# A feed-forward up-projection on one Trainium2 core: half of its columns by seven block products instead of eight

## The chip, the core and the metric

The kernel runs on one core of one Trainium2 chip. The metric is the device time of one execution in microseconds (us). A core has five engines that run side by side, each through its own queue in order: TensorE (PE in the profile, its weight loads PEld), VectorE (DVE), ScalarE (ACT), GpSimd (POOL) and SyncE (SP), which here only issues DMAs. On-chip memory is SBUF (128 partitions) and PSUM, in which TensorE leaves its results: eight banks of 128 x 512 fp32.

## The reference

One encoder layer for 256 tokens of width 2048, all in fp32. Two mixing branches (a retention and a latent attention) are merged and added to the residual `h`; then comes the part that matters here:

```
z = _rmsnorm(h, norm_mlp_g) @ w_up           # (256 x 2048) @ (2048 x 8192)
h = h + square(relu(z)) @ w_down             # (256 x 8192) @ (8192 x 2048)
return _rmsnorm(h, norm_f_g)
```

## The kernel before

**Numbers.** An fp32 operand is split in two parts of TensorE's faster fp32r format: `hi` is the rounded value (ACT copies it, L151 or L216) and `lo` is what the rounding left (DVE subtracts, L152 or L217). A product is then three matmuls: hi by hi, hi by lo and lo by hi.

**Weights.** `weights` (L146) loads a piece of 128 x 1024 numbers (512 KB) into a `raw` tile (5 buffers) through SP's queue, and makes `hi` and `lo` of it (4 buffers each). All weights of the kernel go through this one stream.

**Two forms of a product.** In the *transposed* form (`t_unit`, L170) 128 output columns are made: the weights are the stationary operand and the activations of all 256 tokens move, hi and lo side by side. For each of the 16 blocks of the contraction there is one matmul 512 wide (weight hi by both, `t_pass1`, L159) and one 256 wide (weight lo by hi, `t_pass2`, L163). The result stands transposed (column on the partition, token on the free axis) in two halves of one PSUM bank, and `join` (L204) adds the halves: ACT copies one out (L206), DVE adds (L207). In the *natural* form (`n_tile`, L196; `down`, L807) a tile of 128 tokens is stationary and 512 weight columns move; the three matmuls are each 512 wide.

**Stages around the change.** `w_out` in natural form makes `hn` (L770 to L779: DVE adds the residual, ACT takes the sum of squares). `mlp_turn` (L757) transposes `hn` on TensorE, four 128 x 128 blocks to a PSUM bank, and splits the result into `hT`, scaled by the norm's gain. The up-projection (L785 to L800) is 64 transposed units `z0` to `z63`, each 16 + 16 matmuls; after `join`, DVE makes the squared ReLU in one operation (L800) into `hid`, which stays in SBUF. The down-projection (L819 to L832) runs over the 64 tiles of `hid`: split (`dh`, `dl`), two pieces of `w_down`, and 24 matmuls 512 wide into eight PSUM banks `pd` that are open all the way. Then comes the final norm.

**Memory.** Six SBUF tiles of 16 KB per partition (`big`, L100) hold activations in turn. PSUM is two pools of four banks, `mmps` (L133) and `atps` (L136).

**Order.** The program is traced in the order of the source. A planner then lists each engine's queue: it goes by priority in program order and by the times of its own durations at which operands and buffers come free (`schedule_with_timeline_sim`). On the chip each queue keeps that order.

Of the kernel before, what the change touches and what calls it, by code (L numbers as in the profile page):

```python
# [27 lines left out]
CHUNK = 64  # L28
DFF = 8192
FT = DFF // P  # L30
EPS = 1e-6
QK_SCALE = float(192.0 ** -0.5)
LOWEST = -3.4e38
# [55 lines left out]
def block_kernel(ctx: ExitStack, tc: tile.TileContext, A):  # L89
# [10 lines left out]
    def big(name, dt=F32, shape=(P, KT, S)):  # L100
        return act.tile(list(shape), dt, tag="act16", name=name)
# [31 lines left out]
    def mmps(name):  # L133
        return pmm.tile([P, 512], F32, tag="mm", name=name)
# [61 lines left out]
    def n_tile(out, w, x, t, k0, nk, start, stop):  # L196
        ts = slice(t * P, (t + 1) * P)
        for k in range(nk):
            PE.matmul(out, x.hi(k0 + k, ts), w[0][:, k], start=start and k == 0, stop=False)
            PE.matmul(out, x.lo(k0 + k, ts), w[0][:, k], start=False, stop=False)  # L200
        for k in range(nk):
            PE.matmul(out, x.hi(k0 + k, ts), w[1][:, k], start=False, stop=stop and k == nk - 1)

    def join(out, ps):  # L204
        t = sm.tile([P, S], F32, tag="join", bufs=2, name="join")
# [551 lines left out]
    def mlp_turn(c):  # L757
        for jj in range(2):
            pT = atps(f"ht{c}{jj}")
            for j in range(2):  # L760
                kt = 4 * c + 2 * jj + j
                for t in range(2):
                    o = j * S + t * P
                    PE.transpose(pT[:, o : o + P], hn[:, t, kt * P : (kt + 1) * P], ident)
                g = vec[:, V_MLP + kt : V_MLP + kt + 1]
                split(hT.hi(kt), hT.lo(kt), pT[:, j * S : (j + 1) * S], scale=g)
    hp = ctx.enter_context(tc.tile_pool(name="hp", bufs=1))
    ssh = cp.tile([P, 2, 4], F32, name="ssh")
    rh2 = cp.tile([P, 2], F32, name="rh2")
    for c in range(4):  # L770
        cs = slice(c * 512, (c + 1) * 512)
        pss = [mmps(f"wo{c}{t}") for t in range(2)]
        for kq in range(4):
            n_unit(pss, A["w_out"][4 * c + kq], mg, 4 * kq, 4, kq == 0, kq == 3)
            if kq == 0 and c:
                mlp_turn(c - 1)
        for t in range(2):
            V.tensor_tensor(out=hn[:, t, cs], in0=pss[t], in1=hn[:, t, cs], op=ALU.add)
            SC.activation(pss[t], hn[:, t, cs], AF.Square, accum_out=ssh[:, t, c : c + 1])  # L779
# [2 lines left out]
    V.tensor_scalar(rh2, rh2, 1.0 / D, EPS, op0=ALU.mult, op1=ALU.add)  # L782
    V.reciprocal(rh2, rh2)

    up = [mmps(f"z{i}") for i in range(2)]  # L785
    for i in range(2):
        t_half(up[i], A["w_up"][i], hT, 0)
        if i == 0:
            mlp_turn(3)
    hid = [big(f"hid{i}") for i in range(3)]  # L790
    hid.append(hp.tile([P, KT, S], F32, name="hid3"))
    for i in range(FT):
        if i < 2:
            pz = up[i]
            t_half(pz, A["w_up"][i], hT, 1)
        else:
            pz = mmps(f"z{i}")
            t_unit(pz, A["w_up"][i], hT)
        z = joined(pz)
        V.scalar_tensor_tensor(hid[i // KT][:, i % KT], in0=z, scalar=0.0, in1=z, op0=ALU.max, op1=ALU.mult)  # L800

    pd = [[(mmps if t == 0 else atps)(f"dn{t}{c}") for c in range(4)] for t in range(2)]
    ssf = cp.tile([P, 2, 68], F32, name="ssf")
    rf = cp.tile([P, 2], F32, name="rf")
    LAST = 2

    def down(i, t, c, w, hs):  # L807
        (hi, lo), (dh, dl) = w, hs
        ts = slice(t * P, (t + 1) * P)
        ws = slice(c % 2 * 512, c % 2 * 512 + 512)  # L810
        out = pd[t][c]
        end = i == FT - 1
        mm = tc.keep_in_program_order if i >= FT - LAST else (lambda ins: ins)
        mm(PE.matmul(out, dh[:, ts], hi[:, ws], start=i == 0, stop=False))  # L814
        mm(PE.matmul(out, dh[:, ts], lo[:, ws], start=False, stop=False))  # L815
        mm(PE.matmul(out, dl[:, ts], hi[:, ws], start=False, stop=end))  # L816

    tail = []
    for i in range(FT):  # L819
        dh = hp.tile([P, S], F32R, tag="dh", bufs=3, name=f"dh{i}")  # L820
        dl = hp.tile([P, S], F32R, tag="dl", bufs=3, name=f"dl{i}")
        split(dh, dl, hid[i // KT][:, i % KT])
        ws = []
        for half in range(2):
            w = weights(A["w_down"][i][:, half * 1024 : (half + 1) * 1024], [P, 1024])
            ws.append(w)
            if i < FT - LAST:
                for t in range(2):
                    for c in (2 * half, 2 * half + 1):
                        down(i, t, c, w, (dh, dl))  # L830
        if i >= FT - LAST:
            tail.append((i, ws, (dh, dl)))  # L832
# [7 lines left out]
    def finish(t, c, lo, hi, n):  # L840
        h = hn[:, t, c * 512 + lo : c * 512 + hi]
        ps = pd[t][c][:, lo:hi]
        V.scalar_tensor_tensor(h, in0=ps, scalar=rh2[:, t : t + 1], in1=h, op0=ALU.mult, op1=ALU.add)
        junk = hp.tile([P, 512], F32, tag="junk", bufs=2, name=f"junk{t}{n}")
# [37 lines left out]
def _n_units(w):  # L882
    k, n = w.shape
    u = w.reshape(k // 512, 4, P, n // 512, 512).transpose(3, 0, 2, 1, 4)
    return np.ascontiguousarray(u.reshape(-1, P, 4, 512))


def _cols(v):
# [57 lines left out]
```

## Time and profile before

| | us |
|---|---|
| median of 3 runs (1631.48 to 1631.87) | 1631.72 |
| the profiled execution | 1632.22 |
| its span, first to last instruction | 1630.4 |
| up-projection: first `z` matmul to first `dn` matmul | 915.5 to 1272.7 |
| down-projection: first to last `dn` matmul | 1272.7 to 1620.6 |

The span is shorter than the execution by 1.8 us, which lies around it. TensorE's granted clock has a mean of 0.998 of full speed. In the profile a line `L159 PE MATMUL z<-hT,hi ... x1024 | 245.5, 391` names the source line, engine, operation, the tile written and the tiles read, how many there were, the group's busy time in us and the mean duration of one in ns. TensorE's matmuls overlap: the duration of one is longer than the distance from its start to the next one's start, so rates are read from starts. In the timeline a line is start, duration, engine, line, operation, and in brackets how long the engine had been idle before it and what ended that.

### The profile page before, as it was taken

The page shows a single profiled execution, that of the slowest core. Times are in us where ns is not written, and L with a number is a line of the kernel's source. Part 1 is how long each engine was busy: PE and PEld are TensorE (multiplying, and loading weights), DVE is VectorE, ACT ScalarE, POOL GpSimd, SP SyncE. Part 2 cuts the span into 40 slices and gives each one's busy share as a digit, 9 for nine tenths or more (in the row PEclk, how much of TensorE's full clock was granted, in tenths as well). Part 3 has the DMA queues.
Part 4 walks back from the last instruction along what each step waited for, and adds up shares of the span by engine and source line. Part 5 has one row for each costly group of instructions (what it writes and reads, how often), then busy time and mean ns, then how long its engine had stood idle before and what let it go on. Part 6 is the DMA issues. An engine that isn't in the chain of part 4 may idle for free.

```text
span 1630.4 us, 23041 instructions
## 1 busy us (share of the span) xinstructions
PE 1614.9 (99%) x8782; PEld 1398.8 (86%) x8782; DVE 996.2 (61%) x1491; ACT 809.7 (50%) x1249; POOL 49.5 (3%) x62
## 2 busy tenths in 40 slices
PE   8999999999999999999999999999999999999997
PEld 6888888888889889888888888888888888888886
DVE  7974588655556658666765555555555555555555
ACT  6544555544445556765545544444444444444444
POOL 7100000000000000000000000000000000000001
PEclk9999999999999999999999999999999999999999
DMA  8665544555556554325575555555555655555553
GB/s 306 200 233 193 187 156 166 169 192 186 190 170 203 190 191 146 125 94 176 186 246 187 174 193 188 192 189 186 191 192 184 223 194 192 193 193 195 192 194 112
DMA packets 84480, 304.46 MB, mean 187 GB/s; under 512 B 9360, under 2 KB 9488, under 8 KB 83600
## 3 DMA queue, kind: packets, MB, share of 16 engines
q1 hardware_dynamic: 84368, 302.98, 55.3%
q8 instruction: 69, 1.13, 0.3%
q14 instruction: 43, 0.35, 0.1%
HBM read 300.84 MB, written 2.10 MB: 186 GB/s over the span
## 4 chain that ended last, share of the span: by engine, by line
PE 97%; DVE 1%; issue 0%; DMA 0%; ACT 0%; POOL 0%; SPq 0%; DVEq 0%; POOLq 0%; ACTq 0%
PE z L159 14%; PE z L163 8%; PE dn L816 7%; PE dn L814 7%; PE dn L815 7%; PE rg L159 4%; PE yr L159 4%; PE gr L159 4%; PE gm L159 4%; PE mo L159 4%; PE qk L159 2%; PE gr L163 2%; PE yr L163 2%; PE gm L163 2%; PE rg L163 2%; PE mo L163 2%
## 5 line engine op out<-in xcount | busy, mean ns | idle before, releaser
L152 DVE TENSOR_TENSOR lo<-raw,hi 128x1024 fp32r<-128x1024 f32 (+2 forms) x562 | 666.0, 1204 | 521.6 <-ACT hi L151 248.3
L151 ACT CAST hi<-raw 128x1024 fp32r<-128x1024 f32 (+2 forms) x562 | 580.8, 1035 | 536.9 <-PE z L159 135.2
L159 PE MATMUL z<-hT,hi 128*128 128x512 f32 x1024 | 245.5, 391 | 0.0
L159 PEld LDWEIGHTS z<-hT,hi 128*128 128x128 f32 x1024 | 188.0, 188 | 36.1
L815 PE MATMUL dn<-lo,dh 128*128 128x512 f32 x512 | 199.2, 389 | 0.0
L816 PE MATMUL dn<-hi,dl 128*128 128x512 f32 x512 | 199.2, 389 | 0.0
L814 PE MATMUL dn<-hi,dh 128*128 128x512 f32 x512 | 198.9, 389 | 0.0
L163 PEld LDWEIGHTS z<-hT,lo 128*128 128x128 f32 x1024 | 131.6, 191 | 5.1
L163 PE MATMUL z<-hT,lo 128*128 128x256 f32 x1024 | 133.1, 283 | 0.0
L815 PEld LDWEIGHTS dn<-lo,dh 128*128 128x128 f32 x512 | 96.1, 188 | 20.1
L816 PEld LDWEIGHTS dn<-hi,dl 128*128 128x128 f32 x512 | 96.1, 188 | 19.9
L814 PEld LDWEIGHTS dn<-hi,dh 128*128 128x128 f32 x512 | 96.1, 188 | 19.8
L216 ACT CAST dh<-hid 128x256 fp32r<-128x256 f32 x64 | 26.0, 407 | 89.3 <-PE dn L815 89.3
L159 PE MATMUL mo<-my,hi 128*128 128x512 f32 x256 | 65.5, 396 | 0.4 <-DVE val L207 0.4
L159 PE MATMUL rg<-x,hi 128*128 128x512 f32 x256 | 64.0, 395 | 0.0
L159 PE MATMUL yr<-ry,hi 128*128 128x512 f32 x256 | 61.4, 391 | 0.0
L159 PE MATMUL gr<-x,hi 128*128 128x512 f32 x256 | 61.3, 391 | 0.0
L159 PE MATMUL gm<-x,hi 128*128 128x512 f32 x256 | 61.1, 391 | 0.0
L159 PEld LDWEIGHTS gm<-x,hi 128*128 128x128 f32 x256 | 47.0, 188 | 9.1
L159 PEld LDWEIGHTS gr<-x,hi 128*128 128x128 f32 x256 | 47.0, 188 | 9.0
L159 PEld LDWEIGHTS yr<-ry,hi 128*128 128x128 f32 x256 | 46.9, 188 | 9.0
L159 PEld LDWEIGHTS rg<-x,hi 128*128 128x128 f32 x256 | 46.2, 188 | 8.6
(271 smaller groups left out, 2239.1 us busy)
## 6 DMA issues: line engine op xcount, KB each, us to landing
raw<-w_up SPq DMA_DIRECT2D x128, 512.0 KB, 4.2
raw<-w_down SPq DMA_DIRECT2D x128, 512.0 KB, 4.3
raw<-w_rv SPq DMA_DIRECT2D x32, 512.0 KB, 4.5
raw<-w_rg SPq DMA_DIRECT2D x32, 512.0 KB, 4.5
raw<-w_gret SPq DMA_DIRECT2D x32, 512.0 KB, 4.3
raw<-w_ret_o SPq DMA_DIRECT2D x32, 512.0 KB, 4.6
raw<-w_gmla SPq DMA_DIRECT2D x32, 512.0 KB, 4.4
raw<-w_out SPq DMA_DIRECT2D x32, 512.0 KB, 3.7
```

The lines of the kernel that those rows point to most:

```text
L151: SC.copy(hi, raw)
L152: V.tensor_tensor(out=lo, in0=raw, in1=hi.bitcast(F32), op=ALU.subtract)
L159: PE.matmul(out, w[0][:, k], x.both(k0 + k), start=start and k == 0, stop=False)
L163: PE.matmul(out[:, :S], w[1][:, k], x.hi(k0 + k), start=False, stop=stop and k == n - 1)
L216: SC.copy(hi, val)
L814: mm(PE.matmul(out, dh[:, ts], hi[:, ws], start=i == 0, stop=False))
L815: mm(PE.matmul(out, dh[:, ts], lo[:, ws], start=False, stop=False))
L816: mm(PE.matmul(out, dl[:, ts], hi[:, ws], start=False, stop=end))
```

## The change

The first 4096 of the 8192 columns of `w_up` are made in another form, and the other 32 units stay transposed units.

**Seven products.** For 1024 columns (`u`, four of them) and a pair of contraction blocks (`j`, eight of them) the activations are 2 x 2 blocks of 128 x 128 and the weights 2 x 2 blocks of 128 x 512. A scheme of Strassen's kind (Winograd's form) makes the 2 x 2 product out of seven block products of sums and differences. Each block product is three matmuls 512 wide, so one `s_step` has 21, into seven PSUM banks `qs` (products 3, 4, 2, 5 in `mmps`, 1, 6, 7 in `atps`) that stay open over the eight steps. `s_end` then makes the four output blocks `zo` of the seven banks, once for each `u`: one ACT copy and seven DVE operations of 128 x 512.

**The sums.** Those of the activations (`Combos.make`, four calls, each on DVE two operations of 128 x 1024, the split among them, and four of 128 x 256, and one ACT copy) are made once; two calls stand in the `w_out` stage, two among the first units. Those of the weights are made in every step on DVE: `fa` of 128 x 1024 and `fb` in two operations of 128 x 512. Then three pieces of 128 x 1024 and one of 128 x 512 are split.

**Turn and square.** The output is in natural form, so four turns for each `u` transpose it (four blocks each) in the middle of later steps. Squared ReLU is now two ACT operations (Relu, Square) for both forms, and ACT's queue issues a DMA that stores the tile in DRAM. The down-projection loads each pair of tiles back (`hl`, 3 buffers), first those of the old form, then the others.

**Order and memory.** Three old units come first (`EARLY`), then steps and old units alternate: 32 steps are spread over 27 units, so in five places two steps follow each other; two old units come last (`LATE`). The old units now use `atps` banks. `hn` is saved in DRAM by a DMA from ACT's queue and loaded back at the end of the stage, since its tile is used by `forms`. The sums' hi and lo have five buffers of their own each. The size of a DMA scratch area is reduced.

```diff
+    PRODUCTS = ((3, 0, 0), (4, 0, 1), (2, 1, 0), (5, 1, 1), (6, 2, 0), (1, 2, 1), (7, 3, 0))
...
+    def s_step(qs, src, x, j, between):
+        ra, rb = (wtile("raw", [P, 2, 512]) for _ in range(2))
+        nc.sync.dma_start(ra, src[:, :2])
+        nc.sync.dma_start(rb, src[:, 2:])
+        fa, fb = (forms[:, 2 * (j % 2) + i] for i in range(2))
+        V.tensor_tensor(out=fa, in0=rb[:, 1:].to_broadcast([P, 2, 512]), in1=ra, op=ALU.add)
+        V.tensor_tensor(out=fb[:, 0], in0=fa[:, 0], in1=ra[:, 1], op=ALU.add)
+        V.tensor_tensor(out=fb[:, 1], in0=fb[:, 0], in1=rb[:, 0], op=ALU.add)
+        ws = []
+        for i, r in enumerate((ra, fa, fb, rb[:, :1])):
...
+            split(hi, lo, r)
+            ws.append((hi, lo))
+        for n, (f, i, o) in enumerate(PRODUCTS):
+            if n == 4:
+                between()
+            (ah, al), (hi, lo) = x.get(f, j), ws[i]
+            first, last = j == 0, j == SJ - 1
+            PE.matmul(qs[f], ah, hi[:, o], start=first, stop=False)
+            PE.matmul(qs[f], al, hi[:, o], start=False, stop=False)
+            PE.matmul(qs[f], ah, lo[:, o], start=False, stop=last)
+
+    def s_end(qs, out, tmp):
...
+        SC.copy(t3, qs[3])
+        tt(e, qs[6], t3)
+        tt(f, qs[2], e, ALU.subtract)
+        tt(c21, qs[4], f)
+        tt(c11, qs[5], f)
+        tt(e, e, qs[5], ALU.subtract)
+        tt(c12, qs[1], e)
+        tt(c22, qs[7], t3)
...
+    def square(pair, n, val):
+        t = zp.tile([P, 2, S], F32, tag="hs", bufs=2, name=f"hs{pair}{n}")[:, : val.shape[1]]
+        SC.activation(t, val, AF.Relu)
+        SC.activation(t, t, AF.Square)
+        SC.dma_start(hid[pair][:, n : n + val.shape[1]], t)
...
+    for i in range(EARLY, FT - ST):
+        while done < SU * SJ and done * (FT - ST - EARLY - LATE) <= (i - EARLY) * SU * SJ:
+            next(steps)
+            done += 1
+        pz = atps(f"z{i}")
+        t_unit(pz, A["w_up"][i], hT)
+        square((ST + i) // 2, i % 2, joined(pz).unsqueeze(1))
+    for _ in steps:
+        pass
+    hn = big("hn2", shape=(P, 2, D))
+    nc.sync.dma_start(hn, keep)
...
-    for i in range(FT):
+    for n, i in enumerate((*range(ST, FT), *range(ST))):
+        if n % 2 == 0:
+            hl = hp.tile([P, 2, S], F32, tag="hl", bufs=3, name=f"hl{i}")
+            nc.sync.dma_start(hl, hid[i // 2])
```

More of the change, by code (lines that the diff above doesn't have):

```diff
@@ L30 @@
 FT = DFF // P
+SU = 4
+SJ = KT // 2
+ST = SU * 1024 // P
+EARLY, LATE = 3, 2
+SSF = 68
 EPS = 1e-6
@@ L204, in join, with tt @@
+    def s_end(qs, out, tmp):
+        t3, e, f = (tmp[:, i] for i in range(3))
+        c11, c12, c21, c22 = (out[:, t, c] for t in range(2) for c in range(2))
+        def tt(o, a, b, op=ALU.add):
+            V.tensor_tensor(out=o, in0=a, in1=b, op=op)
+        SC.copy(t3, qs[3])
[6 more added lines that the diff above has]
+        tt(c22, qs[7], t3)
     def join(out, ps):
@@ L776, in block_kernel @@
                 mlp_turn(c - 1)
+        if c in (1, 2):
+            hc.make(c - 1)
         for t in range(2):
@@ L783, in block_kernel @@
     V.reciprocal(rh2, rh2)
-    up = [mmps(f"z{i}") for i in range(2)]
-    for i in range(2):
-        t_half(up[i], A["w_up"][i], hT, 0)
+    hid = [hidd.tile([P, 2, S], F32, name=f"hid{i}") for i in range(FT // 2)]
+    zo = big("zo", shape=(P, 2, 4, 512))
+    def square(pair, n, val):
[3 more added lines that the diff above has]
+        SC.dma_start(hid[pair][:, n : n + val.shape[1]], t)
@@ new lines, in s_units, with turn @@
+    def s_units():
+        turns = []
+        for u in range(SU):
+            qs = {f: (mmps if f in (3, 4, 2, 5) else atps)(f"zs{u}{f}") for f in range(1, 8)}
+            for j in range(SJ):
+                s_step(qs, A["w_up_s"][u, j], hc, j, turns.pop(0) if turns and j else lambda: None)
+                yield
+            s_end(qs, zo[:, 0].rearrange("p (t c) n -> p t c n", t=2), zo[:, 1])
+            def turn(u, jj):
+                pT = atps(f"zt{u}{jj}")
+                for j in range(2):
+                    kt = 2 * jj + j
+                    for t in range(2):
+                        o = j * S + t * P
+                        src = zo[:, 0, 2 * t + kt // 4, kt % 4 * P : kt % 4 * P + P]
+                        PE.transpose(pT[:, o : o + P], src, ident)
+                square(4 * u + jj, 0, pT.rearrange("p (j n) -> p j n", j=2))
+            turns = [lambda u=u, jj=jj: turn(u, jj) for jj in range(4)]
+        for fn in turns:
+            yield
+            fn()
@@ L788, in block_kernel @@
+    forms = None
+    steps = s_units()
+    early = [atps(f"z{i}") for i in range(EARLY)]
+    for i, pz in enumerate(early):
+        t_half(pz, A["w_up"][i], hT, 0)
         if i == 0:
             mlp_turn(3)
-    hid = [big(f"hid{i}") for i in range(3)]
-    hid.append(hp.tile([P, KT, S], F32, name="hid3"))
-    for i in range(FT):
[L793 to L800, printed above, removed]
+            keep = hidd.tile([P, 2, D], F32, name="hnkeep")
+            SC.dma_start(keep, hn)
+            hc.make(2)
+            forms = big("forms", shape=(P, 4, 2, 512))
@@ new lines, in block_kernel @@
+    for i, pz in enumerate(early):
+        t_half(pz, A["w_up"][i], hT, 1)
+        square((ST + i) // 2, i % 2, joined(pz).unsqueeze(1))
+        if i == 0:
+            hc.make(3)
+    done = 0
+    for i in range(EARLY, FT - ST):
[4 more added lines that the diff above has]
+        t_unit(pz, A["w_up"][i], hT)
+        square((ST + i) // 2, i % 2, joined(pz).unsqueeze(1))
@@ L818, in block_kernel @@
     tail = []
-    for i in range(FT):
+    for n, i in enumerate((*range(ST, FT), *range(ST))):
+        if n % 2 == 0:
+            hl = hp.tile([P, 2, S], F32, tag="hl", bufs=3, name=f"hl{i}")
+            nc.sync.dma_start(hl, hid[i // 2])
         dh = hp.tile([P, S], F32R, tag="dh", bufs=3, name=f"dh{i}")
         dl = hp.tile([P, S], F32R, tag="dl", bufs=3, name=f"dl{i}")
-        split(dh, dl, hid[i // KT][:, i % KT])
+        split(dh, dl, hl[:, i % 2])
         ws = []
```

61 lines of the change are left out of this document (53 added, 8 removed).

## The prediction

> **What bounds the kernel now.** First the busy totals of the page, then the table by stage, then the timeline of two ordinary units.
>
> ```profile
> PE 1614.9 (99%) x8782; PEld 1398.8 (86%) x8782; DVE 996.2 (61%) x1491; ACT 809.7 (50%) x1249; POOL 49.5 (3%) x62
> ...
> 915.00:1272.00 357.00, 357.00 (x2054) 315.26 (x2053) 202.05 (x267) 162.52 (x203) 0.00 (x0) 1.00 0.56 189
> 1272.00:1620.00 348.00, 348.00 (x1540) 288.26 (x1540) 186.62 (x201) 155.07 (x201) 4.40 (x4) 1.00 0.56 187
> ```
>
> The stage lines hold the length and then the busy time of PE, PEld, DVE, ACT, POOL, the granted clock and the DMA share. In the up-projection (915 to 1272) PE is busy all the time at full clock, DVE 202 of 357 us, ACT 163, DMA 0.56: TensorE alone sets the end.
>
> ```profile
> 1004.76 2.36 DVE L152 TENSOR_TENSOR lo<-raw,hi 128x1024 fp32r<-128x1024 f32 x2 [2.41 <-PE z L163]
> 1005.46 3.82 PE L159 MATMUL z<-hT,hi 128*128 128x512 f32 x16
> 1005.66 0.37 ACT L206 COPY join<-z 128x256 f32<-128x256 f32 x1 [0.87 <-PE z L163]
> 1007.04 0.42 DVE L207 TENSOR_TENSOR val<-z,join 128x256 f32<-128x256 f32 x1
> 1007.49 0.42 DVE L800 SCALAR_TENSOR_TENSOR hid<-val 128x256 f32<-128x256 f32 x1
> 1009.11 2.08 PE L163 MATMUL z<-hT,lo 128*128 128x256 f32 x16
> 1011.03 1.32 PE L159 MATMUL z<-hT,hi 128*128 128x512 f32 x5
> ```
>
> Starts give the rates. Sixteen 512-wide matmuls take 1009.11 - 1005.46 = 3.65 us (228 ns each), sixteen 256-wide 1.92 us (120 ns): a unit is 5.57 us. DVE waits 2.41 us for PE to free a buffer: it is ahead, and has room.
>
> **What TensorE gains.** Thirty-two units go: 32 x 5.57 = 178.2 us. In come 4 x 8 steps of 21 matmuls 512 wide with activations stationary, the form of the down-projection:
>
> ```profile
> L814 PE MATMUL dn<-hi,dh x512: 389/389/396, 1272.7 to 1620.2; 128*128 128x512 f32 x171
> ...
> L816 PE MATMUL dn<-hi,dl x512: 388/389/389, 1273.1 to 1620.6; 128*128 128x512 f32 x171
> ```
>
> First to last start: (1620.6 - 1272.7) / 1535 = 226.6 ns. A step is 4.76 us, 32 steps 152.3: 25.9 us less. The 64 new transposes are priced by those of `hn`:
>
> ```profile
> 852.74 0.60 PE L764 MATMUL ht<-con,hn 128*128 128x128 f32 x4
> 853.10 0.48 PE L199 MATMUL wo<-hi,mg 128*128 128x512 f32 x1
> 853.41 0.40 PE L200 MATMUL wo<-hi,mg 128*128 128x512 f32 x1
> ```
>
> Four take 0.36 us, and the matmul behind them 0.31 instead of 0.23: 0.44 a turn, 16 turns 7.1 us. Net on TensorE: 25.9 - 7.1 = **18.8 us less**, a stage of 338.4 for 357.2. This holds if PE never waits.
>
> The Trainium skill ("TensorE: Matmul & The Clock Gate", section "Back-to-back issue gap") gives the isolated distance of matmuls at full clock as N/2.4 + 2.5 ns. That is 215.8 for 512 and 109.2 for 256; by it the estimate would be 166.4 - 145.0 = 21.4 saved instead of 25.9. The rows are slower than the rule in both forms, and more so in the form that goes.
>
> **What VectorE gets.** Distances between starts where DVE has no gap, from the end of the previous stage and the start of this one:
>
> ```profile
> 931.48 1.22 DVE L152 TENSOR_TENSOR lo<-raw,hi 128x1024 fp32r<-128x1024 f32 x1
> 932.61 0.42 DVE L800 SCALAR_TENSOR_TENSOR hid<-val 128x256 f32<-128x256 f32 x1
> 932.95 0.42 DVE L207 TENSOR_TENSOR val<-z,join 128x256 f32<-128x256 f32 x1
> ...
> L778 DVE TENSOR_TENSOR hn<-wo,hn x8: 683/688/692, 846.5 to 915.7; 128x512 f32<-128x512 f32 x8
> ```
>
> An operation of 128 x 1024 lasts 1.22 but the next starts after 1.13; 128 x 256 lasts 0.42 and occupies 0.34; 128 x 512 lasts 0.69 and, by the same 0.09, occupies 0.60. An operation that needs the one before it waits the full duration and 0.03 more (L207 to L800 above: 0.45). So a step is `fa` 1.25 + `fb` 0.72 + 0.60 + three splits of 1.13 + one of 0.60 = 6.56 us, against 4.76 of PE: **DVE can't feed steps alone**. A unit is 2.27 + 0.42 = 2.7 (the squared ReLU leaves DVE) against 5.57. `s_end` is seven operations, mostly in a chain, 4.6; each `make` 4.0. The stage: 32 x 6.56 + 32 x 2.7 + 4 x 4.6 + 2 x 4.0 + 3.8 (`hT`, `hn`, the sums) = 326.5 us against PE's 338.4: **DVE is 96% full**, where it was 57%.
>
> ACT: steps 32 x (3 x 1.05 + 0.62) = 121; units 32 x (2.10 + 0.37 + two squares' halves at 0.41) = 105; turns 16 x 1.2 = 19; the rest 7; 48 DMA issues at the 0.33 that SP's take = 16. That is 268 of 338, 79%. Queued behind each store on ACT are the next `hi` copies, for which DVE's `lo` waits; the 70 us of room cover it. If ACT were late, DVE would be, and PE with it.
>
> **Where PE will wait.** A wait can't be below nothing, and nothing in the sum is saved twice, so these only take from 18.8.
> - Start. Three early units and `mlp_turn` give PE 17.6 us. DVE has in that time six `lo` 6.8, three joins 1.2, two `make` 8.0 and 3.8 of the rest: 19.8, and then the first step's 6.6, of which the first products need 1.1. `forms` also waits until `hn` is stored: 2 MB, by `hn<-x` 8.8 us to landing, by the slower `xn<-x` (1 MB) 12.9; it ends about when needed. Between 0 and 5 us; I take 3.
> - Ends of a `u`. 4.6 us of DVE come at once. An old unit stands between, so the banks are free in time; DVE's lead, about 2 us with these buffers, and 0.65 of room in each pair of step and unit leave up to 2. Three inner ends: 0 to 6; I take 4.
> - Turns. Products 1, 6, 7 hold three `atps` banks, so units and turns share one. After a unit PE has four products (2.7 us) until the turn: ACT's copy (up to 1.05 behind another, then 0.37) and DVE's add (up to 1.13, then 0.42) make up to 3.0, typically 2. After the turn three products (2.0 us) cover Relu (up to 1.05, then 0.6). 16 turns, I take 0.1 each, 2; the far end is a rival.
> - End of the stage: four last turns and their banks before `pd`: 0 to 2; I take 1.
>
> Sum 10: a stage of 348.5, 8.8 us less than before.
>
> **Edits at nothing.** The two `make` in `w_out`: DVE is busy there 50 of 91 us; they borrow two of five `raw` buffers, and the three left hold 3 x 2.7 us of matmuls against 3.7 to landing. Without that cover, up to 4 us each. Storing and loading `hid`: 256 KB lands in 2.5 us (`out<-hn`), the first `hl` was stored hundreds of us earlier, and DMA has 0.44 of its time free; if not, a few us at the join of the stages. Reloading `hn` has the whole down-projection; SP's `raw` loads are queued behind it, and it waits for a freed tile, which the planner places after the combos' last use; five loaded buffers cover it. The scratch size moves no instruction.
>
> From the execution's 1632.2: 1632.2 - 18.8 + 10 = 1623.4; the median of the runs lies 0.5 below the profiled one, so **1623**.
>
> **Rivals.**
> 1. *All waits hidden*: 1631.7 - 18.8 = 1613, up to 1618. For it: in 15 to 25 us of the span DVE was busy 5.00 of every 5.00 us, so it can run without a gap. Against it: 4% of room.
> 2. *DVE becomes the bound.* Without the overlap of 0.09 between operations, because waits on ACT stand between them, the durations count: steps 32 x 6.95, units 32 x 2.87, `s_end` 4 x 4.8, the rest 12.3: 346 us, 8 above PE's sum; with gaps of 1 to 4% 350 to 360, against 357. Time 1624 to 1635, middle 1629. For it: such an order alternates ACT and DVE in every split. The Trainium skill ("VectorE: DVE Perf Modes", section "The DRAIN you can't avoid") says that the next operation starts only when the pipe is empty, and in the next section that an operation which isn't held starts earlier; the pairs of `lo` above (two in 2.36, not 2.45) agree with the exception.
> 3. *Slower, by the shared bank.* The queues' order is fixed beforehand. If on DVE a unit's `join` stands behind a step's block of forms and splits, rather than behind one operation, the bank comes free 0.2 + 1.4 + (3 to 6.6) + 0.4 after the unit, 2.3 to 5.9 us after PE wants it. The point from which it decides is 18.8 / 16 = 1.2 us a turn, less what the other waits took: 0.5. At 1.5 to 2.5 in each of 16 turns, 24 to 40 us: 1637 to 1660, middle 1645. Against it: the planner's queue puts a ready `join` first, as 933 us shows, where `join` came between two `lo`.
>
> That PE's products aren't seven but as slow as eight is excluded by counts: 672 matmuls of a known rate.
>
> **How the numbers follow.** Forecast (waits 5 to 14) 0.45; rival 1 0.12; rival 2 0.20; rival 3 0.23. The measurement tells about 0.2%, 3.3 us, from no change. Faster by more than that (below 1628.4): all of rival 1, the forecast, and a little of rival 2: 0.60. Within: 0.13. Slower: rival 3 and the end of rival 2: 0.27. The range 1613 to 1645 leaves out the upper half of rival 3 and the end of rival 1. Within the sign that I forecast, 1613 to 1628.
>
> **What would show it.** The `zs` matmuls' starts 227 ns apart, 672 of them; the up-projection about 348 us; PE's idle time named after DVE `lo`, `forms` or `val`, some 10 us, clustered at the start and at the three ends of a `u`; DVE's busy time in the stage 320 to 330. A stage below 343 is rival 1; DVE without gaps and PE waiting all along is rival 2; PE waiting at the turns' `zt` for `val`, over 1 us each, is rival 3. Waits outside the stage, in `w_out` or the down-projection, would make the forecast wrong in a place that I priced at nothing.

## The result and the profile after

| | before | after |
|---|---|---|
| median (runs) | 1631.60 us (4) | 1646.20 us (4, 1644.47 to 1648.04) |
| ratio | | 1.0091, 95% interval 1.0075 to 1.0107: 0.9% slower |
| profiled execution, its span | 1632.22, 1630.4 | 1647.19, 1645.4 |
| first `z` to first `dn` | 357.2 | 370.8 |
| first to last `dn` | 347.9 | 350.7 |

The forecast was 1623 in a range of 1613 to 1645. The time went the other way, 14.6 us up, and lies 1.2 us outside the range. The up-projection was to become 348.5 us; it is 370.8, and the down-projection gave 2.8 more.

The busy totals of the page after:

```profile
PE 1610.9 (98%) x8494; PEld 1374.6 (84%) x8494; DVE 1118.6 (68%) x1607; ACT 888.2 (54%) x1385; POOL 49.8 (3%) x62
```

TensorE has 288 matmuls fewer, but the span is longer. The stages, with the same columns as in the prediction (length, busy time of PE, PEld, DVE, ACT, POOL, clock, DMA share, GB/s):

```profile
915.00:1285.00 370.00, 349.54 (x1761) 290.25 (x1760) 315.84 (x366) 232.88 (x327) 0.00 (x0) 0.99 0.67 222
1285.00:1636.00 351.00, 349.70 (x1543) 288.33 (x1541) 184.77 (x200) 159.99 (x211) 4.78 (x5) 1.00 0.65 207
```

PE was busy for all of 357 us before; now it idles 20 of 370, while DVE has gone from 202 to 316 busy and still has 54 free. No engine is full: the loss is waiting. A stretch of TensorE's timeline shows that the matmuls cost what was said where nothing waits:

```profile
1149.41 0.39 PE L266 MATMUL zs<-shi,hc 128*128 128x512 f32 x1
1149.64 0.39 PE L265 MATMUL zs<-shi,hc 128*128 128x512 f32 x1
1149.86 0.39 PE L266 MATMUL zs<-shi,hc 128*128 128x512 f32 x1
```

Starts are 0.23 apart. What is new is in the groups (operation, count, busy time and mean ns of one, idle time before them):

```profile
L265 PE MATMUL zs<-shi,hc 128*128 128x512 f32 x96 | 39.0, 406 | 6.8 <-ACT shi L297 6.1 <-DVE zo L274 0.7
L266 PE MATMUL zs<-shi,hc 128*128 128x512 f32 x96 | 37.9, 395 | 0.0
```

PE idles mostly ahead of the *first* matmul that needs a step's split weights (L265; L266, which follows it, has no idle time). Its waits in the stage, by what ended them (total, times, longest):

```profile
PE zs L265 <- ACT shi L297: 6.1, 6, 3.0
PE z L164 <- ACT hs L877: 3.8, 5, 1.2
PE zs L267 <- DVE lo L298: 2.4, 4, 1.1
PE zs L265 <- ACT hi L297: 2.2, 3, 1.3
PE zs L267 <- DVE slo L298: 1.4, 3, 0.6
...
PE zt L897 <- ACT hs L877: 1.2, 1, 1.2
...
PE z L164 <- DVE val L288: 0.2, 1, 0.2
```

No name holds most of it. **To add it up without names**, take each distance between two starts on TensorE, subtract the rate of the first (0.228 and 0.120 in a unit, 0.2266 in a step, 0.44 for a turn), and sum from the first `z` to the last instruction of the stage. Before, that sum is -1.0; after, it is **32.1 us**, where the prediction had 10. The gaps over 0.7 us, sorted by the wait that ended them: start of the stage 3.0; splits of a step (`shi`, `slo`, `hi`, `lo`) away from the start 8.7; the shared bank after a turn (`hs`) 5.2; ends of a `u` 1.9. The other 13 are in gaps under 0.7. The sum also holds what a lower granted clock took, since the rates are those of the full clock; in the kernel after that is about 3 us, by an estimate from the clock rows at the end of this document.

The worst place shows how one wait leads to the next (start, duration, engine, and in brackets the wait):

```profile
1152.71 0.33 SPq L245 DMA_DIRECT2D raw<-w_up_s  x1
...
1154.40 0.60 PE L897 MATMUL zt<-con,zo 128*128 128x128 f32 x4
...
1155.85 0.59 ACT L877 ACTIVATE hs<-zt 128x512 f32<-128x512 f32 x1
...
1156.50 0.66 PE L897 MATMUL zt<-con,zo 128*128 128x128 f32 x4 [1.23 <-ACT hs L877]
...
1157.78 1.23 DVE L247 TENSOR_TENSOR forms<-raw,raw 128x1024 f32<-128x1024 f32 x1 [1.93 <-DMA raw<-w_up_s]
...
1159.04 1.04 ACT L297 CAST shi<-forms 128x1024 fp32r<-128x1024 f32 x1 [1.94 <-DVE forms L247]
...
1160.14 0.79 PE L265 MATMUL zs<-shi,hc 128*128 128x512 f32 x1 [2.99 <-ACT shi L297]
```

Two turns stand with one matmul between them. Both need the one bank that the products leave, so the second waits until Relu has emptied it. TensorE's queue then stands at a step whose weights were asked for at 1152.71 and landed at about 1157.7; one sum on DVE and one copy on ACT later TensorE goes on, 3 us late. The granted clock was 0.67 in the 5 us behind this place (same columns as the stages; the clock is the third figure from the end):

```profile
1155.00:1160.00 5.00, 0.92 (x6) 0.42 (x4) 3.07 (x3) 3.03 (x5) 0.00 (x0) 0.98 0.93 345
1160.00:1165.00 5.00, 4.86 (x15) 3.90 (x16) 3.71 (x5) 2.72 (x5) 0.00 (x0) 0.67 0.64 217
1165.00:1170.00 5.00, 5.00 (x31) 4.44 (x30) 2.16 (x3) 2.38 (x4) 0.00 (x0) 1.00 0.03 7
```

At the end of the stage, ACT stands for a store (`hs` has two buffers), and TensorE for ACT:

```profile
1287.10 0.84 ACTq L879 DMA_DIRECT2D hid<-hs  x2
...
1292.92 0.60 ACT L877 ACTIVATE hs<-zt 128x512 f32<-128x512 f32 x1 [5.33 <-DMA hid<-hs]
...
1293.57 0.50 PE L948 MATMUL dn<-hi,dh 128*128 128x512 f32 x1 [0.95 <-ACT hs L877]
...
1296.95 0.50 PE L948 MATMUL dn<-hi,dh 128*128 128x512 f32 x1 [0.35 <-ACT hs L877]
```

The first `dn` matmuls wait twice for a bank that Relu has to empty, and Relu for the store. The two places cost 1.6 us over the rate, and the last turn, which now stands among the `dn` matmuls, 0.4: most of the 2.8 us that the down-projection became longer.

### The profile page after: what moved, and what is told of

Same layout as the page of the kernel before. It is cut to its first block, busy times and chain, and to the rows that moved or that the text cites. A ratio compares the mean times of both kernels' runs of the same rounds, so it can differ in the third digit from the quotient of the medians.

```text
span 1645.4 us, 22858 instructions
## 1 busy us (share of the span) xinstructions
PE 1610.9 (98%) x8494; PEld 1374.6 (84%) x8494; DVE 1118.6 (68%) x1607; ACT 888.2 (54%) x1385; POOL 49.8 (3%) x62
## 5 line engine op out<-in xcount | busy, mean ns | idle before, releaser
L157 DVE TENSOR_TENSOR lo<-raw,hi 128x1024 fp32r<-128x1024 f32 (+2 forms) x498 | 591.1, 1202 | 378.9 <-ACT hi L156 246.0
L156 ACT CAST hi<-raw 128x1024 fp32r<-128x1024 f32 (+2 forms) x498 | 512.3, 1032 | 421.3 <-PE dn L950 95.3
L164 PE MATMUL z<-hT,hi 128*128 128x512 f32 x512 | 125.8, 397 | 5.3 <-ACT hs L877 3.8
L164 PEld LDWEIGHTS z<-hT,hi 128*128 128x128 f32 x512 | 96.7, 191 | 28.5 <-ACT hs L877 5.9
L297 ACT CAST shi<-forms 128x1024 fp32r<-128x1024 f32 x64 | 66.9, 1049 | 33.4 <-DVE forms L247 21.4
L298 DVE TENSOR_TENSOR slo<-forms,shi 128x1024 fp32r<-128x1024 f32 x64 | 77.9, 1219 | 5.9 <-ACT shi L297 5.9
L168 PEld LDWEIGHTS z<-hT,lo 128*128 128x128 f32 x512 | 66.2, 191 | 2.8
L168 PE MATMUL z<-hT,lo 128*128 128x256 f32 x512 | 67.2, 283 | 0.0
L297 ACT CAST hi<-raw 128x1024 fp32r<-128x1024 f32 x64 | 52.9, 834 | 26.3 <-PE z L164 15.4
L298 DVE TENSOR_TENSOR lo<-raw,hi 128x1024 fp32r<-128x1024 f32 x64 | 59.7, 952 | 3.4 <-PE z L168 3.0
```

Source lines behind the costliest of these rows:

```text
L156: SC.copy(hi, raw)
L157: V.tensor_tensor(out=lo, in0=raw, in1=hi.bitcast(F32), op=ALU.subtract)
L164: PE.matmul(out, w[0][:, k], x.both(k0 + k), start=start and k == 0, stop=False)
L168: PE.matmul(out[:, :S], w[1][:, k], x.hi(k0 + k), start=False, stop=stop and k == n - 1)
```

## The experiments

The expectations name theories by letters. The missing time is due to: **A** too few `raw` buffers; **B** stores that hold ACT through the two `hs` buffers; **C** DVE being nearly full; **D** the loads of `hl` standing early in SP's queue; **E** an order planned with loads that land sooner than they do; and, formed on the traces with three and two `u`, **F** the one PSUM bank that units and turns share.

"Lost" is the sum defined above, from each kernel's profiled execution, as is the last column; the median is that of all runs. Where the text says how many of TensorE's 8494 matmuls "moved", it is the smallest number that has to change places to turn one trace's order of starts into the other's.

| kernel | median us | ratio to before (95%) | lost us | first `z` to last `dn` |
|---|---|---|---|---|
| after | 1646.2 | 1.0091 (1.0075 to 1.0107) | 32.1 | 721.5 |
| four store buffers | 1640.8 | 1.0057 (1.0042 to 1.0072) | 28.8 | 715.9 |
| `hl` loads late | 1659.1 | 1.0173 (1.0156 to 1.0190) | 43.8 | 732.8 |
| six `raw` buffers | 1646.6 | 1.0090 (1.0075 to 1.0105) | 30.3 | 717.6 |
| no sums on DVE | 1644.1 | 1.0079 (1.0064 to 1.0094) | 31.4 | 719.2 |
| steps' weights loaded once | 1643.2 | 1.0070 (1.0055 to 1.0085) | 28.2 | 716.7 |
| three `u` | 1672.3 | 1.0252 (1.0234 to 1.0269) | 55.0 | 747.0 |
| two `u` | 1708.4 | 1.0470 (1.0454 to 1.0486) | 83.1 | 780.6 |
| TensorE in program order | 1669.4 | 1.0228 (1.0212 to 1.0244) | 50.2 | 737.8 |
| six product banks | 1631.3 | 0.9998 (0.9989 to 1.0008) | 15.8 | 703.9 |
| six banks, two `u` | 1635.4 | 1.0018 (1.0008 to 1.0027) | 8.7 | 705.7 |
| join by ACT | 1654.6 | 1.0137 (1.0122 to 1.0153) | 38.0 | 727.3 |
| join by ACT, two `u` | 1688.1 | 1.0349 (1.0331 to 1.0366) | 60.6 | 757.6 |
| turns together | 1666.1 | 1.0211 (1.0196 to 1.0226) | 54.4 | 740.9 |
| same, four store buffers | 1663.0 | 1.0190 (1.0175 to 1.0205) | 46.9 | 733.4 |
| six banks, four store buffers | 1630.2 | 0.9995 (0.9985 to 1.0006) | 15.7 | 703.1 |
| same, no sums on DVE | 1641.0 | 1.0058 (1.0039 to 1.0078) | 28.3 | 715.5 |
| half banks | 1652.5 | 1.0134 (1.0117 to 1.0151) | 24.1 | 722.5 |
| seventh product apart | 1640.7 | 1.0062 (1.0048 to 1.0076) | 26.6 | 714.0 |

### Buffers and loads

**Four store buffers.**

```diff
-        t = zp.tile([P, 2, S], F32, tag="hs", bufs=2, name=f"hs{pair}{n}")[:, : val.shape[1]]
+        t = zp.tile([P, 2, S], F32, tag="hs", bufs=4, name=f"hs{pair}{n}")[:, : val.shape[1]]
```

> The store's tile hs gets four buffers instead of two; nothing else is changed. Theory B (two store buffers: Relu waits on ACT until a store has landed, 4 to 6 us, and holds a PSUM bank and ACT's queue meanwhile) expects the 7.9 us of PE's gaps that end with hs in the up-projection and the 2.8 us that the down-projection became longer to go, and some that hang on them: 1632 to 1637. Theory A (five raw buffers are too few, so that VectorE stands for loads) expects the 2.8 us at the stage's end at most: 1642 to 1645. Theory C (VectorE, 96% full, can absorb no wait from anywhere) expects the same as A.

It took 5.4 us off, less than B expected and more than A and C, 2.2 of them in the down-projection (348.5). Only some 45 matmuls moved, so this is the cleanest of the edits: the stores were a cause, and about a third of the loss against before.

**Late `hl` loads.**

```diff
-            nc.sync.dma_start(hl, hid[i // 2])
+            tc.keep_in_program_order(nc.sync.dma_start(hl, hid[i // 2]))
```

> The loads of hl are kept behind all loads of the up-projection in SP's queue; three of them stood early in it, where SP waited 11.3 us in all for stores. Theory D (weight loads are late because SP waits behind those) expects the waits of the stage's first 60 us to shrink by about 5: 1640 to 1642. Theories A, B and C expect less than 3: 1643 to 1647.

Up to the last `z` the stage is as long as before the edit (368.2 for 369.4 us); then the first `dn` matmul waits 11.9 us for `dh`, since the loads now come too late. Where they had stood had cost little. D falls.

**Six `raw` buffers.**

```diff
-        dt, bufs = (F32, 5) if kind == "raw" else (F32R, 4)
+        dt, bufs = (F32, 6) if kind == "raw" else (F32R, 4)
```

> Six raw buffers instead of five. Theory A expects VectorE's 26.5 us of waits for loads to fall to a third and PE's gaps that end with shi, slo or lo, 15 us, to halve: 1634 to 1639. Theory B expects no change beyond 2 us: 1644 to 1647. Theory C expects a small gain: 1641 to 1645.

Nothing changed in the time, though some 220 matmuls moved. DVE waited 29.2 us for the steps' loads, where it had waited 26.5: a sixth buffer doesn't shorten that wait, and A falls as it was drawn.

**Weights of the steps loaded once** (two loads fewer in every later step; the two tiles that hold them take room, so four `raw` buffers are left for the units).

```diff
-        dt, bufs = (F32, 5) if kind == "raw" else (F32R, 4)
+        dt, bufs = (F32, 4) if kind == "raw" else (F32R, 4)
...
-        ra, rb = (wtile("raw", [P, 2, 512]) for _ in range(2))
-        nc.sync.dma_start(ra, src[:, :2])
-        nc.sync.dma_start(rb, src[:, 2:])
+        if not held:
+            held.extend(zp.tile([P, 2, 512], F32, name=f"held{i}") for i in range(2))
+            nc.sync.dma_start(held[0], src[:, :2])
+            nc.sync.dma_start(held[1], src[:, 2:])
+        ra, rb = held
```

> The steps' weights are loaded once and used in all 32 steps (the output is not the reference's): 62 of the up-projection's 128 loads are left out, VectorE, ScalarE and TensorE do all their work. Theory E expects the waits that hang on step loads to go, 20 of 32 us: up-projection 350, time 1625 to 1632. Theory C expects little: 1641 to 1646. Theory B (stores) expects its 5 to stay in both.

3 us. The DMA share of the stage fell to 0.38, and 28.2 us are still lost. So the late landing in the timeline above is one link of that chain; without any late step load nearly as much is lost, by other waits. E falls as the one cause.

### VectorE's load

The three sums of a step are left out.

```diff
-        V.tensor_tensor(out=fa, in0=rb[:, 1:].to_broadcast([P, 2, 512]), in1=ra, op=ALU.add)
-        V.tensor_tensor(out=fb[:, 0], in0=fa[:, 0], in1=ra[:, 1], op=ALU.add)
-        V.tensor_tensor(out=fb[:, 1], in0=fb[:, 0], in1=rb[:, 0], op=ALU.add)
...
-        for i, r in enumerate((ra, fa, fb, rb[:, :1])):
+        for i, r in enumerate((ra, ra, rb, rb[:, :1])):
```

> The three operations on VectorE that make the weights' sums are left out, and loaded pieces are split in their place (the output is not the reference's). VectorE loses 32 x 2.57 = 82 us of the stage's 327. Theory C expects the gaps at steps to go and the stage to come near 345: 1617 to 1624. Theory A expects half of the gaps at steps to stay, since pieces are held shorter but the loads are as many: 1630 to 1636. Theory B expects the 10 us at stores to stay: 1633 to 1638.

The same 350 us of the kernel after, of this one, and of the one with weights loaded once:

```profile
915.00:1265.00 350.00, 329.54 (x1645) 272.56 (x1644) 301.79 (x349) 221.83 (x310) 0.00 (x0) 0.99 0.66 219
```

```profile
915.00:1265.00 350.00, 329.99 (x1649) 274.68 (x1647) 229.43 (x253) 217.38 (x310) 0.00 (x0) 0.99 0.66 221
```

```profile
915.00:1265.00 350.00, 332.88 (x1663) 277.82 (x1662) 302.45 (x351) 222.42 (x311) 0.00 (x0) 0.98 0.38 128
```

DVE (third busy time) has 72 us less to do in the second line, and PE is busy 0.45 us more. The time is 20 us above C's range, and above A's and B's too: taking work off DVE doesn't bring the time down, so C falls as the one cause. The edit does more than that, though. A step's first copy on ACT (`shi`) now reads the loaded piece itself, and waited 56.3 us for loads, so this kernel may stand at another limit; what a lighter DVE is worth by itself, it doesn't tell.

### Fewer steps

```diff
-SU = 4
+SU = 3
```

> Three of the eight blocks of columns in the new form instead of four (24 steps over 35 units). By the rows PE's sum of the up-projection is 343 us and VectorE's 291 (85% instead of 96%). Theory C (VectorE's fill decides) expects most of the waits to go: up-projection 350, time 1624 to 1630. Theory E (waits come with each step, about 1 us, because the queues' order is planned with loads that land sooner than on the chip, whatever room VectorE has) expects 24 us of waits: up-projection 367, time 1639 to 1644.

> Two of eight blocks in the new form (16 steps over 43 units). PE's sum is 348 us, VectorE's 256 (73%). Theory C expects 2 to 4 us of waits: up-projection 351, time 1624 to 1628. Theory E expects 16 us of waits: 364, time 1636 to 1641.

Both are far outside what C and E expected: with three and two `u`, DVE's load falls (250 and 203 of the same 350 us), and the time *rises*, to 1672 and 1708. The trace with two `u` shows a unit straight behind a unit, which the kernel after hardly has:

```profile
994.84 2.07 PE L168 MATMUL z<-hT,lo 128*128 128x256 f32 x16
...
996.95 0.37 ACT L287 COPY join<-z 128x256 f32<-128x256 f32 x1 [0.86 <-PE z L168]
...
998.33 0.42 DVE L288 TENSOR_TENSOR val<-z,join 128x256 f32<-128x256 f32 x1
...
998.80 1.48 PE L164 MATMUL z<-hT,hi 128*128 128x512 f32 x5 [1.89 <-DVE val L288]
```

The bank of the first unit must be joined before the second can begin. From the first unit's last phase to the second's first matmul it is 3.96 us, for 1.92 of work: **2.04 us for handing the bank over**. That is theory F. TensorE's largest waits in this kernel, by name; `val` is the bank's, `shi` and `slo` are a step's splits:

```profile
PE zs L265 <- ACT shi L297: 17.1, 10, 3.3
PE z L164 <- DVE val L288: 14.1, 9, 1.9
PE zs L267 <- DVE slo L298: 10.1, 10, 1.8
PE zt L897 <- DVE val L288: 5.1, 4, 1.9
```

### TensorE in program order

Every matmul of a step and a unit, and every turn, is pinned to the order of the source.

```diff
-            PE.matmul(qs[f], ah, hi[:, o], start=first, stop=False)
+            pin(PE.matmul(qs[f], ah, hi[:, o], start=first, stop=False))
...
-                        PE.transpose(pT[:, o : o + P], src, ident)
+                        pin(PE.transpose(pT[:, o : o + P], src, ident))
```

> TensorE's queue is kept in the order of the source from the first step on: steps and units whole, none mixed. If the waits come from products that the planner put ahead of a ready unit, they go by half: 1630 to 1638. If what is late is the supply of sums and splits itself (theory C), a whole unit no longer fills a step's wait and the time rises or stays: 1645 to 1655.

18 us more lost, and 23.2 us more time with the same work and the same buffers, beyond both numbers expected: the order alone is worth that much. Now the shared bank's own names carry the waits, as the prediction's rival 3 drew them:

```profile
PE zt L901 <- DVE val L292: 11.3, 6, 3.1
PE z L168 <- DVE val L292: 9.5, 7, 2.6
PE zs L271 <- DVE slo L302: 4.4, 3, 2.2
PE zs L269 <- DVE zo L278: 4.1, 4, 2.4
```

Free to choose, the planner puts matmuls of later products in these places. The likely reading is that it escapes the wait for `val` at the price of standing at a step's splits earlier, which is where the kernel after shows its waits; the two traces fit it, and the next runs test it.

### A second bank

Product 7 is added into product 1's bank: TensorE's instructions are the same, and two banks are left for units and turns.

```diff
-            qs = {f: (mmps if f in (3, 4, 2, 5) else atps)(f"zs{u}{f}") for f in range(1, 8)}
+            qs = {f: (mmps if f in (3, 4, 2, 5) else atps)(f"zs{u}{f}") for f in range(1, 7)}
+            qs[7] = qs[1]
...
-            first, last = j == 0, j == SJ - 1
+            first, last = j == 0 and f != 7, j == SJ - 1 and f != 1
```

> Product 7 is added into the bank of product 1 (the output is not the reference's); every engine has the same instructions, but the steps hold six PSUM banks, and units and turns share two instead of one. Theory F (the one bank that units and turns share sets the order of TensorE's queue and its waits; a unit straight behind a unit costs 2.04 us) expects 10 to 20 of the 32 us of waits to go: up-projection 350 to 360, time 1625 to 1636. Theories C and E, in which sums and loads come late, expect 1642 to 1647.

> Two of eight blocks in the new form, with product 7 in the bank of product 1 (output not the reference's). With one shared bank this division took 1708 us. Theory F expects that a second bank takes nearly all of it away: up-projection 350 to 356, time 1625 to 1632, better than any so far. Theories C and E expect 1690 or more.

With four `u` 14.9 us less than the kernel after, as F expected; with two `u` 72.9 less than its counterpart, 3.4 above F's range and 55 below the other theories'. TensorE's waits with two `u`, all of them:

```profile
PE zs L265 <- ACT shi L297: 1.9, 1, 1.9
PE zs L265 <- ACT hi L297: 1.4, 1, 1.4
PE zs L267 <- DVE slo L298: 1.1, 1, 1.1
PE z L164 <- ACT hi L156: 0.6, 1, 0.6
PE z L164 <- DVE hT L301: 0.6, 1, 0.6
```

Not only `val` is gone; the 17.1 us for `shi` and 10.1 for `slo` are 1.9 and 1.1. Waits that bear a split's name went with the bank. For two `u` theory F is shown. The Trainium skill ("Perfetto Trace Analysis", section "Matmuls") asks for just this, that independent groups of matmuls rotate through different banks, so that emptying one lies beside filling the next; the two runs agree, by 72.9 us. The bank is enough to explain four `u` too, but a new order was drawn along with it: some 380 matmuls moved.

With four store buffers added:

> Product 7 in product 1's bank (output not the reference's), and four store buffers. With two it took 1631.3. Theory B for the rest: 4 to 6 us less, 1625 to 1627. If the stores only cost where the bank was short: 1629 to 1632.

1630.2: four store buffers are worth 5.4 us where the bank is short, and 1.1, within the scatter of the runs, where it isn't. Then the sums on DVE are left out as well:

> As six_hs4, and the three sums of the weights on VectorE left out (output not the reference's). Theory C, hidden so far behind the bank: the waits left, about 10 us, go too and the up-projection nears 341: 1615 to 1619. If VectorE's fill isn't the cause: within 3 us of six_hs4.

This is outside both expectations. With a second bank and 81 us less on DVE the time went *up* by 10.8 us, and 28.3 are lost. Two things changed. Some 290 matmuls moved. And what stood for the loads is another engine, for much longer; first a line of the kernel with sums, then one of the kernel without (total, times, longest):

```profile
DVE forms L247 <- DMA raw<-w_up_s: 24.6, 18, 3.9
```

```profile
ACT shi L294 <- DMA raw<-w_up_s: 85.9, 45, 6.5
```

With the sums, their first one waits for the load on DVE; without them, ACT's first copy does, and all of ACT's queue behind it. Whether the order or these waits took the 10.8 us, no run here separates. Since the kernel in program order shows that an order alone can be worth 23 us, differences of some 10 us between two edits that re-draw it say little by themselves.

### Handing the bank over sooner

ACT copies the whole bank, so that DVE's addition isn't needed to free it.

```diff
+        if whole[0]:
+            SC.copy(t, ps)
+            V.tensor_tensor(out=out, in0=t[:, :S], in1=t[:, S:], op=ALU.add)
+            return
```

> From the first step on, a unit's join copies the whole bank out with one ACT operation of 128 x 512 (about 0.6 us instead of 0.37) and DVE adds the halves in SBUF, so that the shared bank is free without DVE. Theory F expects 4 to 10 us less: 1636 to 1642. Theories C and E expect no change or 1 us more, for ACT's longer operation: 1645 to 1648.

> Two of eight blocks in the new form, with the join's copy of the whole bank by ACT. Theory F: a unit straight behind a unit waits about 1 us instead of 2: 1708 falls by 20 to 40, to 1668 to 1688. Theories C and E: 1705 to 1710.

With two `u` 20 us came back, at the edge of what F expected; with four `u` it is 8.4 us slower than the kernel after, against what F expected, and 38.0 us are lost. There the order put the first `dn` ahead of the last unit; what made it slower isn't shown.

All four turns of a `u` together, straight behind `s_end` (first as it is, then with four store buffers):

```diff
-                s_step(qs, A["w_up_s"][u, j], hc, j, turns.pop(0) if turns and j else lambda: None)
+                s_step(qs, A["w_up_s"][u, j], hc, j, lambda: None)
...
-            turns = [lambda u=u, jj=jj: turn(u, jj) for jj in range(4)]
-        for fn in turns:
-            yield
-            fn()
+            for jj in range(4):
+                turn(u, jj)
+            yield
```

> The four turns of a block stand together right after its end, when the seven banks are free, and no longer in the middle of the next block's steps; nothing else is changed. If the turns are the dear users of the shared bank, 10 to 14 of the 32 us go: 1632 to 1637. If the units are, little changes: 1642 to 1648.

> The same, and four store buffers instead of two. The two effects add: between0's time less 4 to 6, so 1627 to 1632 if the turns are dear, 1637 to 1642 if the units are. Below 1628 it would beat both kernels.

20 and 17 us slower than the kernel after, both outside what was expected. The four turns follow each other on one bank, `s_end` has to be finished for them, and the next step waits for `s_end` too (`zo` below). How the 20 us divide isn't shown. The largest waits of the first of the two:

```profile
PE zs L267 <- DVE lo L298: 7.9, 9, 2.3
PE zs L265 <- DVE zo L274: 6.0, 3, 3.4
PE zs L265 <- ACT shi L297: 4.8, 5, 1.9
```

### A second place without leaving anything out

**Half banks.** Units and turns in halves of the one bank, with four store buffers.

```diff
+    def h_unit(out, src, x):
...
+            for k in range(HK):
+                kk = half * HK + k
+                PE.matmul(out, hi[:, k], x.hi(kk), start=kk == 0, stop=False)
+                PE.matmul(out, hi[:, k], x.lo(kk), start=False, stop=False)
...
+        return halves[0][:, nh[0] % 2 * S : nh[0] % 2 * S + S]
```

> A second place in the one free bank, with nothing left out of the computation: from the fourth old unit on, a unit is made in half a bank (256 columns) by three matmuls 256 wide for each of its 16 blocks, so that units and turns take the two halves of the bank in turn, and a unit needs no join at all; turns become half turns of two transposes, at two points of a step; store buffers are four. TensorE's sum grows: 29 units x 16 x (3 x 120 - 348 = 12 ns) = 5.6 us, and the half turns some 1.3, together 7 against the kernel with four store buffers (1640.8). Theory F (the one bank for units and turns is what the time goes to): the 10.6 us that a second bank brought to the kernel with four store buffers come back: 1633 to 1639. Rival (the second bank helped only because another queue order was drawn, or one half can't be filled while the other is read): no gain, only the 7: 1646 to 1655.

1652.5, in the rival's range. The loss went from 28.8 us to 24.1, by less than the 7 us of added work; the rest of the 11.7 between the two medians isn't accounted for. The trace shows that the premise was wrong:

```profile
1148.67 0.38 PE L906 MATMUL halves<-con,zo 128*128 128x128 f32 x2
...
1149.09 0.38 ACT L889 ACTIVATE hs<-halves 128x256 f32<-128x256 f32 x1 [1.08 <-PE halves L906]
...
1149.52 0.44 PE L906 MATMUL halves<-con,zo 128*128 128x128 f32 x2 [0.47 <-ACT hs L889]
```

The second half turn starts only when Relu has read the *other* half: in this program a bank is one place, however it is cut. The Trainium skill ("PSUM — Partial Sum Buffer", section "PSUM bank collisions raise a hardware error") gives a reason for such waits: two engines must not access one bank on the same partitions at once, disjoint columns included. The wait of 0.47 us agrees with a program that keeps to it; what happens without the wait, no run here shows.

**The seventh product apart.** Product 7 leaves the steps and is made once for each `u` as a unit of 24 matmuls in a shared bank; ACT copies it out, and the last addition of `s_end` takes it.

```diff
+                if j == 5:
+                    s_seventh(atps(f"zs{u}7"), zo[:, 0, 3], u, hc)
+                    yield
...
-        tt(c22, qs[7], t3)
+        tt(c22, c22, t3)
```

> A second bank with nothing left out: of the seven products, product 7 leaves the steps (18 matmuls each, into six banks) and is made once for each 1024 columns as a unit of its own, 24 matmuls 512 wide in one of the two shared banks, behind the sixth step; ACT copies its bank to SBUF, where the last addition takes it. TensorE does the same 672 matmuls. Its weights are loaded a second time (8 MB more in all, on a DMA share of 0.66), VectorE's splits are the same columns in fewer operations, ACT does four copies more. Store buffers are four. Theory F (the one bank for units and turns is what the time goes to, whatever order is drawn): near the kernel with six banks and four store buffers, 1626 to 1634, TensorE's waits in the up-projection 10 to 18 us. Rival (six banks gained by the order that was drawn, not by the bank): near the kernel with four store buffers alone, 1638 to 1650, waits of 25 or more.

1640.7, the rival's number, 0.1 us from the kernel with four store buffers. It isn't a clean test. This kernel asks for 8 MB more and has four store buffers, and ACT's waits in the stage are new ones (in the kernel after the same two names have 4.4 and 4.1 us):

```profile
ACT hi L156 <- DMA raw<-w_up: 28.6, 19, 3.0
ACT hi L311 <- DMA raw<-w_up_s: 17.3, 11, 3.2
```

ACT waits 46 us for weights where it waited 8.5. Either that ate the bank's gain, or at four `u` the bank gains less than the six-bank kernels show; this run can't tell. No version without anything left out was faster than before; the best are this one and the one with four store buffers, both 0.6% slower.

## Why the prediction was wrong

**TensorE's sum, right.** 672 matmuls came in, and where nothing waits they start 0.23 us apart; with the loss taken off, the stage is 370.8 - 32.1 = 338.7 for the 338.4 predicted. As the loss is counted from the prediction's own rates, this confirms the counts and that no other work stands in the stage. TensorE has 18.8 us less to do, as predicted.

**VectorE's and ScalarE's load, nearly right.** 316 us busy for 320 to 330; ScalarE 233, where 252 were worked out besides the DMA issues. Rival 2 had DVE without gaps, and it idles 54 us of the stage: it isn't the bound. How much its fill adds to the waits stays open, since the kernels without sums stand for loads instead.

**The failed step: "Where PE will wait", a sum of 10.** By its items, in gaps over 0.7 us: start 3.0 for 3; ends of a `u` 1.9 for 4; turns 5.2 for 2 ("16 turns, I take 0.1 each"). The items that were named came out near their sum, 10.1 for 9. What was missing is a term for *ordinary steps*: 8.7 us of visible waits for a step's splits and 13 in small gaps; the end of the stage, taken at 1, cost 2.8, in the down-projection. The prediction had let DVE run ahead there because its total fitted. A total of 96% says nothing of when an operation stands in its queue: DVE waited 26.5 us in 17 places for weights to land, and ACT 21.4 for DVE's sums. No one of these waits is the cause: with the steps' loads left out, 28.2 us were still lost. Of the 13 in small gaps, about 3 are the halved clock (estimate below).

**An edit priced at nothing: storing `hid`.** DMA's free time was named as its cover, and it wasn't the issue. The buffer was: `hs` has two, a store took 3.8 us (128 KB) or 4.7 (256 KB) to land in the median, ACT's queue stood behind it for up to 5.33, and four buffers take 5.4 us off where the bank is short. ACT's "70 us of room" is no cover for a queue that goes in order.

**Rival 3, by its number but not by its sign.** Its middle of 1645 was 1 us from the result. Its sign, PE waiting at the turns for `val` by over 1 us each, isn't there: for `val` units waited 0.2 us in all, and one turn 1.2, for Relu. The bank it named is the strongest cause that the runs found (14.9 and 72.9 us when a second is free), but with a planner that may move other products ahead, the wait for the bank seems to turn into waits for splits: with the order pinned the sign is there. And the prediction gave the bank to 16 turns alone; all 29 units after the first three hand it on as well.

**What stays open.** How the 32 us at four `u` divide between the bank and the drawn order. Two edits that free a bank by adding two products into one give 15.8 and 15.7 lost. Two others that free a bank, one of them with no sums besides and one with the seventh product apart, give 28.3 and 26.6, and in both ACT stands for loads (85.9 and 46 us): the loads may be the next limit behind the bank, which no run here tests. The kernels with one shared bank in which only store or `raw` buffers, the steps' loads or the sums were changed lie at 28.2 to 32.1. That the planner's order went wrong because its durations differ from the chip's is argued, not shown.

## What to carry to other kernels

Count PSUM banks before matmuls: a scheme that keeps seven of eight open leaves one for everything else, and each thing made in it waits for its reader (2.04 us from unit to unit here), whatever the engines' totals say. Where queues are planned, look for such a wait not only under the bank's name: the cheapest test is a second bank, or the same program in source order. And if an edit re-draws the order, compare it with several other edits that do so before believing a difference of 10 us, and look at what stands for the loads in each.

## What was not expected of the hardware

- The granted clock was halved for 3.4 us in two places of the otherwise full stage of the kernel after, each behind a cluster of short waits: 0.50 from 968.7 to 972.1 and from 1159.9 to 1163.2. By these rows that is about 3 of the 32.1 us lost (an estimate). Six `raw` buffers, with 30.3 us lost, had 1.00 from 915 to 1265, so not every such wait does it. With two `u` the clock was 0.94 on average over the same 350 us; by that some 21 of its 83.1 us lost are the clock itself (an estimate), on top of the waits.
- Fewer steps, hence more of the old work, made the kernel slower by 26 and 62 us. With two `u`, where old units stand next to each other, a second bank took that away; for three `u` the same cause is likely, and not tested.
